# Down-projection weights kept as a bf16 copy in DRAM, and deeper prefetch around the norms, in a two-layer mLSTM/attention trunk

## The chip, the cores and the metric

One Trainium2 chip, one program on all 8 NeuronCores (two dies: cores 0 to 3 and 4 to 7). Each core computes one sequence of the batch, nothing is exchanged. The metric is the device time of the slowest core in microseconds. Executions come in two kinds. In *fast* ones every core holds nearly the full TensorE clock (a mean of 0.96 to 0.98 in the kernel before); in *slow* ones the cores of one die or of both are granted less (means down to 0.80). A ratio of two kernels here is the mean time of one kernel's fast runs over that of the other's fast runs of the same rounds, so it is not quite the ratio of the medians that are quoted beside it.

Because an execution can be slow in one stage and undisturbed in another, I also give *stage lengths at full clock*: from the first matmul of a stage to the first of the next, core by core, and the median over those cores whose record shows no throttling (a granted clock of about 0.81) in that stage. They can be compared between runs whose total times cannot.

The clock records hold three values: 1, 0.8125 (0.81 in the views) and 0.5. The last is the half clock of the prediction. On core 4 of the kernel before it is read from 1383.4 to 1407.3 us, around PE's waits of 6.8 and 13.2 us at the head of layer 0's first up stage.

## The reference, cut to what matters

Two layers. Layer 0 mixes tokens with an mLSTM, layer 1 with dilated sliding-window attention; after each comes a gated ConvFFN. Every sub-layer starts with an RMSNorm (with a scale and a shift from a conditioning vector) and ends with a residual add.

```python
for i in range(DEPTH):                       # 2
    h = rms_norm(x, norm_mix[i]) * (1.0 + sc_m) + sh_m
    y = mlstm_mixer(...) if i % 2 == 0 else dilated_mixer(...)
    x = x + g_m * y                          # y ends with "@ w_out", 2048 x 2048
    h = rms_norm(x, norm_ffn[i]) * (1.0 + sc_f) + sh_f
    x = x + g_f * conv_ffn(h, ...)           # up 2048 x 11264, conv, gate, down 5632 x 2048
return rms_norm(x, norm_out)
```

D = 2048, 2048 tokens a core, D_FF = 5632. All weights arrive as f32; the matmuls run on bf16 or f16.

## The kernel before

A recorder puts instructions on the five engines in program order and derives the semaphores. POOL, which computes and issues loads, and DVE work through their lists in that order (in the timeline that the prediction shows, POOL's add starts at 7901.47 us after a wait of 14.68 us, and its four loads only at 7902.68; DVE's eviction starts at 7899.73, behind a norm tile that waited 4.19 us). The stages are: prologue, mLSTM, output projection 0, FFN 0 (up, down for tokens 0 to 1023; up, down for 1024 to 2047), attention, output projection 1, FFN 1 (the same four). "First" and "second" up and down mean these token halves. The activations of a half stay in SBUF, so the down weights pass three times: once in the first down stage, twice in the second, which does one 512-token tile at a time.

The ring of weight slabs: six slots; POOL (GpSimd) issues a load as soon as PE has released a slot. The down slabs are cast from f32 to bf16 by the DMA itself.

```python
def load(self):                              # class slabs, cut
    ...
    if kind == "u":
        self.c.R.dma("pool", self.t[...][:], self.c.T["f_wu"][self.l, a, b], ...)
    else:
        self.c.R.dma("pool", self.td[...][:], self.c.T["f_wd"][self.l, a, b], ...)
```

Down stage, cut. Per output tile: 44 matmuls, eviction on DVE, square on ACT, row sum on POOL, then two or three steps of `bg`, the norm of the other token half, which runs in the shadow of this stage.

```python
for n_, (fo, ss) in enumerate(order):
    for q in range(4):
        w = ring.get(...)
        ...                                   # 11 matmuls per token tile
        ring.done()                           # POOL: loads the next slabs
    for s_ in ss:
        if m + 1 < 32: ldx(m + 1)             # residual, one tile ahead
        R.stt(n, PS[...], gcol[...], xin[m % 2][:], ALU.mult, ALU.add)      # DVE
        ...
        R.act(sq[m % 2][:], n, AF.Square)                                   # ACT
        R.tt("pool", a[:], a[:], sq[m % 2][:], ALU.add)                     # POOL
        bg = pull(bg, 2 if tb == 0 else 3)    # norm tiles: load, DVE, then ACT or a store
```

The norm loads one tile ahead into `len(xr)` buffers, two of them:

```python
    ld(0)
    for fc in range(16):
        if fc + 1 < 16: ld(fc + 1)
        R.stt(x[:], x[:], gvec[...], rstd, ALU.mult, ALU.mult)
        ...                                   # ACT into hT or B; in the last stage a store to outT
        yield
```

The output projections use the same pattern: residual and result on two buffers each, and the norm of the first token half beside the second half's matmuls.

The softmax here doesn't subtract the row's maximum and nothing guards it: scores larger than these inputs give would overflow.

## Time and profile before

| | us |
|---|---|
| five timed runs before the change was tried | 7680, 8241, 8354, 8452, 8489; median 8353.61 |
| profiled run (slow): die 0, die 1 | 8118, 8336 |
| output projections, full clock | 247.5 and 258.4 |
| first up stages | 554.0 and 554.1 |
| first down stages | 310.8 and 310.6 |
| second up stages | 536.1 and 536.0 |
| second down stages | 414.4 and 442.8 |

The stage rows are medians over undisturbed cores, layer 0 first. (The last second down stage also holds the 19 us end of the program.) The lines of the profile are shown in the prediction and not repeated.

### The profile page before, as it was taken

How to read it: one execution, taken by the hardware profiler on the slowest of the kernel's cores; microseconds unless marked ns; L12 is line 12 of the kernel's file. 1: busy time of each engine (PE TensorE's matmuls, PEld its weight loads, DVE VectorE, ACT ScalarE, POOL GpSimd, SP SyncE). 2: the span in 40 equal slices, each digit the busy share in tenths (PEclk: the TensorE clock that was granted, in tenths of full speed). 3: DMA queues.
4: the chain of work that ended last, by engine and by line, in shares of the span. 5: the costliest groups of instructions: out<-in, count | busy, mean ns of one | idle time of the engine just before them, and what ended most of it. 6: DMA issues, size and time to landing. Idle time of an engine off the chain costs nothing.

```text
span 8352.0 us, 123527 instructions; the slowest of 8 cores (8106.8 to 8352.0 us)
## 1 busy us (share of the span) xinstructions
PE 7827.3 (94%) x44026; PEld 4252.0 (51%) x44216; DVE 3892.7 (47%) x6968; ACT 2383.5 (29%) x4525; POOL 2107.6 (25%) x2931
## 2 busy tenths in 40 slices
PE   2799998999999888999999999999999999999978
PEld 2466653444444335776666666666434443444433
DVE  1656645883388422443333333433246661377511
ACT  2644433442144212222222222222133331133300
POOL 1322222222222222332222222222322221222222
PEclk9899999999999999998888888888778888888877
DMA  9067656556755795232222221111454446544588
GB/s 187 12 109 123 107 126 156 88 87 131 149 87 87 139 197 117 52 54 49 42 48 49 41 49 24 31 31 24 113 160 71 72 71 138 113 71 71 87 180 167
DMA packets 275358, 774.66 MB, mean 93 GB/s; under 512 B 30272, under 2 KB 31808, under 8 KB 268608
## 3 DMA queue, kind: packets, MB, share of 16 engines
q0 software_dynamic: 151056, 541.20, 38.9%
q1 hardware_dynamic: 123696, 225.54, 8.7%
q8 instruction: 361, 5.91, 0.3%
q14 instruction: 245, 2.01, 0.1%
HBM read 1229.37 MB, written 78.38 MB: 157 GB/s over the span
## 4 chain that ended last, share of the span: by engine, by line
PE 82%; DMA 9%; DVE 4%; issue 2%; ACT 2%; POOL 1%; another core or an unknown queue 0%; SPq 0%; DVEq 0%; ACTq 0%; POOLq 0%
PE PS L209 82%; DMA f_nx<-xb 2%; DMA outT<-f_nx 2%; DMA o_h<-xa 1%; DMA f_down<-f_wd 1%; DMA f_r<-sums 1%; DMA s_wa<-w_ada 1%; DMA o_x<-xT 0%; DMA f_x<-xb 0%; POOL s_scr L227 0%; DVE f_tv L223 0%; DVE f_tg L223 0%; DMA o_x<-xb 0%; DMA m_wab<-w_ada 0%
## 5 line engine op out<-in xcount | busy, mean ns | idle before, releaser
L209 PE MATMUL PS<-a_wa,hT 128*128 128x384 bf16 x12288 | 2421.0, 361 | 17.2 <-DVE a_R L237 17.2
L209 PEld LDWEIGHTS PS<-a_wa,hT 128*128 128x128 bf16 x12288 | 1455.8, 121 | 774.5 <-issue 22.5
L209 PE MATMUL PS<-f_act,f_down 128*128 128x512 bf16 x5516 | 1380.0, 415 | 104.9 <-DMA f_down<-f_wd 93.5
L209 PE MATMUL PS<-B,f_up 128*128 128x512 f16 x5632 | 1438.8, 408 | 7.0 <-DVE o_n L223 6.8
L209 PE MATMUL PS<-B,f_ws 128*128 128x512 f16 x4224 | 1103.3, 409 | 22.4 <-DVE f_ws L227 22.4
L209 PEld LDWEIGHTS PS<-f_act,f_down 128*128 128x128 bf16 x5632 | 587.1, 105 | 902.3 <-issue 594.4
L209 PEld LDWEIGHTS PS<-B,f_up 128*128 128x128 f16 x5632 | 582.0, 103 | 774.0 <-issue 443.6
L219 ACT ACTIVATE a_qkv<-PS 128x384 bf16<-128x384 f32 x768 | 377.1, 491 | 1999.1 <-PE PS L209 1999.1
L237 DVE COPY a_R<-PS 128x64 f32<-128x64 f32 x768 | 172.5, 225 | 1399.7 <-ACT a_qkv L219 1399.5
L209 PEld LDWEIGHTS PS<-B,f_ws 128*128 128x128 f16 x4224 | 437.1, 104 | 601.4 <-issue 354.4
L209 PE MATMUL PS<-m_wkvo,hT 128*128 128x320 bf16 x4096 | 622.2, 304 | 0.0
L227 POOL TENSOR_TENSOR f_act<-f_tg,f_tv 128x1024 bf16<-128x1024 f32 x176 | 413.4, 2349 | 713.1 <-DVE f_tv L223 538.7
L227 POOL TENSOR_TENSOR a_tA<-a_R,a_cs 128x128 f32<-128x128 f32 x384 | 174.7, 455 | 1362.5 <-DVE a_R L237 1335.0
L223 DVE SCALAR_TENSOR_TENSOR f_tv<-PS,f_cw,f_tv 128x1023 f32<-128x1023 f32 x352 | 451.1, 1281 | 141.8 <-ACT f_tv L219 119.7
L209 PE MATMUL PS<-yT,o_w 128*128 128x512 bf16 x2006 | 494.4, 411 | 14.1 <-DVE o_n L223 6.0
L227 DVE TENSOR_TENSOR PS<-PS,f_p 128x512 f32<-128x512 f32 x528 | 359.7, 697 | 284.4 <-PE PS L209 283.3
L209 PEld LDWEIGHTS PS<-m_wkvo,hT 128*128 128x128 bf16 x4096 | 401.7, 101 | 154.7 <-issue 1.8
L219 ACT ACTIVATE f_p<-PS 128x512 f32<-128x512 f32 x528 | 314.5, 596 | 570.6 <-PE PS L209 497.5
L223 DVE SCALAR_TENSOR_TENSOR f_tg<-PS,f_cw,f_tg 128x1023 f32<-128x1023 f32 x352 | 450.2, 1279 | 55.1 <-ACT f_tg L219 36.5
L204 POOL DMA_DIRECT2D f_up<-f_wu x352 | 197.4, 561 | 1067.6 <-PE PS L209 1041.2
L219 ACT ACTIVATE f_tg<-PS,f_cb,f_cw 128x1024 f32<-128x1024 f32 x176 | 212.0, 1205 | 766.2 <-DVE PS L227 766.2
L204 POOL DMA_DIRECT2D f_down<-f_wd x384 | 208.1, 545 | 720.5 <-PE PS L209 700.2
(184 smaller groups left out, 7406.7 us busy)
## 6 DMA issues: line engine op xcount, KB each, us to landing
f_up<-f_wu POOLq DMA_DIRECT2D x352, 512.0 KB, 5.1
f_down<-f_wd POOLq DMA_DIRECT2D x384, 352.0 KB, 7.4
a_wa<-a_wi POOLq DMA_DIRECT2D x48, 1536.0 KB, 10.5
m_wab<-w_ada POOLq DMA_DIRECT2D x64, 512.0 KB, 6.2
xa<-o_n SPq DMA_DIRECT2D x128, 256.0 KB, 2.3
f_x<-xa SPq DMA_DIRECT2D x128, 256.0 KB, 6.5
a_wab<-w_ada POOLq DMA_DIRECT2D x64, 512.0 KB, 5.2
xb<-f_n SPq DMA_DIRECT2D x96, 256.0 KB, 5.9
```

The lines of the kernel that those rows point to most:

```text
L204: self.q[eng].append((ws, lambda e, o=out, i=in_: e.dma_start(out=o, in_=i), sem))
L209: return self.op("pe", lambda e: e.matmul(out, lhsT=lhsT, rhs=rhs, start=start, stop=stop, **kw), [out], [lhsT, rhs])
L219: return self.op("act", lambda e: e.activation(**kw), outs, ins)
L223: return self.op("dve", lambda e: e.scalar_tensor_tensor(out=out, in0=in0, scalar=scalar, in1=in1, op0=op0, op1=op1), [out], ins)
L227: return self.op(eng, lambda e: e.tensor_tensor(out=out, in0=in0, in1=in1, op=op), [out], [in0, in1])
L237: return self.op(eng, lambda e: e.tensor_copy(out=out, in_=in_), [out], [in_])
```

## The change

The intent: load the down weights as bf16 by casting them once into DRAM, so that the second down stages stop being short of DMA; and give the norms and residuals around the matmul stages more buffers and earlier loads. Cut to its core (left out: new buffer addresses, one buffer for the squares of a down stage instead of two, and residual loads issued just after an eviction instead of just before it):

```diff
+    T["wdb"] = nc.dram_tensor("wdb", [2, 16, 4, 128, 11, 128], BF16, kind="Internal").ap()
@@ mLSTM, attention, first up stage of layer 0: one cast at a time
+def cast_down(c, l):
+    for fo in range(16):
+        for q in range(4):
+            c.R.dma("pool", c.T["wdb"][l, fo, q], c.T["f_wd"][l, fo, q], f"cast{q}", dw=[("wdb", l, fo, q)])
+            yield
@@ slabs.load
-            self.c.R.dma("pool", self.td[...][:], self.c.T["f_wd"][self.l, a, b], ...)
+            self.c.R.dma("pool", self.td[...][:], self.c.T["wdb"][self.l, a, b], ..., dr=[("wdb", self.l, a, b)])
@@ norm_tiles: loads len(xr) // 2 ahead
-    ld(0)
+    ah = len(xr) // 2
+    for fc in range(ah):
+        ld(fc)
     for fc in range(16):
-        if fc + 1 < 16:
-            ld(fc + 1)
+        if fc + ah < 16:
+            ld(fc + ah)
@@ phase_out: four buffers for residual, result and norm; residual three ahead
-    rst0, nx = hs[2:4], hs[4:6]
+    rst0, nx = hs[2:4], hs[4:6] + [... two more ...]
-    ldx(0)
+    for i in range(3):
+        ldx(i)
@@ phase_out, second token half, output tile 14: the first weight sums of the up stage
+                if fo == 14:
+                    first_sums(c, l)
@@ phase_ffn, norm of the other half
-            yield
-            yield
+            for _ in range(4):
+                yield
             rstd_of(c, rst[:], rst[:], ...)
-            yield from norm_tiles(c, n_li, n_src, tq, rst[:], nx, [0])
+            yield from norm_tiles(c, n_li, n_src, tq, rst[:], nx + xn if l == 1 and tb == 1 else nx, [0])
@@ phase_ffn, residual: three buffers, two ahead
-        ldx(0)
+        for i in range(2):
+            ldx(i)
```

More of the change, by code (lines that the diff above doesn't have):

```diff
@@ L167, in dma @@
         ins = [] if dr is None or dr else [in_]
-        if dw:
+        if in_.tensor.name in self.dram_names:
+            ins = []
+        elif dw:
             ins = [in_]
-        elif in_.tensor.name in self.dram_names:
-            ins = []
         val = self.dsem.get(sem, 0) + 16
@@ L840, in phase_mlstm @@
     feeder, bg = feeds(), ada_bg()
+    cast = cast_down(c, 0)
     for s in range(N + 2):
@@ L875, in phase_mlstm @@
                 M.load_w(h + 1, (tt // 3,))
+        if 2 <= s < 26:
+            cast = pull(cast)
+        c.cast0 = cast
         if s == 111:
@@ L945, in phase_out @@
     src, dst, li = (("xT", "xa", 2), ("xb", "xa", 3))[l]
-    XR = c.R2 + kb(64.25)
-    xin = [R.sb(f"o{l}_x{i}", [128, 512], F32, XR + 2048 * i) for i in range(2)]
-    xn = [R.sb(f"o{l}_n{i}", [128, 512], F32, XR + 4096 + 2048 * i) for i in range(2)]
+    xin = [R.sb(f"o{l}_x{i}", [128, 512], F32, a) for i, a in enumerate(
+        [c.HA + 2048 * k for k in range(4)] + [c.R1 + 4096 * k for k in (6, 7, 8, 9)])]
+    xn = [R.sb(f"o{l}_n{i}", [128, 512], F32, a) for i, a in enumerate(
+        [c.HA + kb(8) + 2048 * k for k in range(4)] + [c.R1 + 4096 * k for k in (10, 11, 12, 13)])]
+    xi = lambda m: m % 4 + 4 * (m >= 35)
     acc0 = [R.sb(f"o{l}_a{k}", [128, 512], F32, c.HA + kb(56) + 2048 * k) for k in range(2)]
-    sq = [R.sb(f"o{l}_q{k}", [128, 512], F32, c.HA + kb(60) + 2048 * k) for k in range(2)]
+    sq = [R.sb(f"o{l}_q{k}", [128, 512], F32, a) for k, a in enumerate((c.HA + kb(60), c.HA + kb(62), c.R1 + 4096 * 14, c.R1 + 4096 * 15))]
     hs = [R.sb(f"o{l}_h{k}", [128, 512], F32, c.R1 + 4096 * k) for k in range(6)]
     acc = [acc0, hs[0:2]]
-    rst0, nx = hs[2:4], hs[4:6]
+    rst0, nx = hs[2:4], hs[4:6] + [R.sb(f"o{l}_h{k}", [128, 512], F32, c.R2 + kb(54 + 2 * k)) for k in (6, 7)]
     xcnt = [0]
@@ L961, in ldx @@
         tq = tb * 2 + sub
-        R.dma("sp", xin[m % 2][:], T[src][:, fo, tq * 512:(tq + 1) * 512], f"xin{m % 2}", dr=[(src, fo, tq)])
-    ldx(0)
+        R.dma("sp", xin[xi(m)][:], T[src][:, fo, tq * 512:(tq + 1) * 512], f"xin{m % 4}", dr=[(src, fo, tq)])
+    for i in range(3):
+        ldx(i)
     bg = None
@@ L973, in phase_out @@
                     R.mm(PS[:, bk, :], W.w[fo][:, kc, :], c.yT[:, kc, sl], kc == 0, kc == 15)
-                if m + 1 < 64:
-                    ldx(m + 1)
-                n = xn[m % 2]
-                R.stt(n[:], PS[:, bk, :], gcol[:, fo:fo + 1], xin[m % 2][:], ALU.mult, ALU.add)
-                R.dma("sp", T[dst][:, fo, sl], n[:], f"st_x{m % 2}", dw=[(dst, fo, tq)])
+                n = xn[xi(m)]
+                R.stt(n[:], PS[:, bk, :], gcol[:, fo:fo + 1], xin[xi(m)][:], ALU.mult, ALU.add)
+                if m + 3 < 64:
+                    ldx(m + 3)
+                R.dma("sp", T[dst][:, fo, sl], n[:], f"st_x{m % 4}", dw=[(dst, fo, tq)])
                 a = acc[tb][sub]
@@ L982, in phase_out @@
                 else:
-                    q = sq[m % 2]
+                    q = sq[m % 2 + 2 * (m >= 35)]
                     R.act(q[:], n[:], AF.Square)
@@ L1002, in phase_out, with weight_sums, first_sums @@
         R.dma("sp", T["sums"][2 + sub], acc[1][sub][:], f"sums{sub}", dw=[("sums", 2 + sub)])
+def cast_down(c, l):
[3 more added lines that the diff above has]
+            yield
+def weight_sums(c, S, wg, wv, halves=(0, 1)):
+    R = c.R
+    a11, a12, a21, a22 = wg[:, 0:8, :], wg[:, 8:16, :], wv[:, 0:8, :], wv[:, 8:16, :]
+    if 0 in halves:
+        R.tt("dve", S[:, 0], a21, a22, ALU.add)
+        R.tt("dve", S[:, 1], S[:, 0], a11, ALU.subtract)
+    if 1 in halves:
+        R.tt("dve", S[:, 2], a12, S[:, 1], ALU.subtract)
+        R.tt("dve", a21, a11, a21, ALU.subtract)
+def first_sums(c, l):
+    c.wsum = [c.R.sb(f"f{l}_ws{i}", [128, 3, 8, 128], F16, (c.HA + kb(56), c.R2 + kb(60))[i]) for i in range(2)]
+    weight_sums(c, c.wsum[0], c.ring.get(0), c.ring.get(1))
 class slabs:
@@ L1009, in __init__ @@
         R = c.R
-        at = [c.R2 + kb(24) + 4096 * i for i in range(self.NR)]
-        self.t = [R.sb(f"f{l}_up{i}", [128, 16, 128], F16, a) for i, a in enumerate(at)]
-        self.td = [R.sb(f"f{l}_down{i}", [128, 11, 128], BF16, a) for i, a in enumerate(at)]
+        self.t = [R.sb(f"f{l}_up{i}", [128, 16, 128], F16, c.R2 + kb(24) + 4096 * i) for i in range(self.NR)]
+        self.td = [R.sb(f"f{l}_down{i}", [128, 11, 128], BF16, c.R2 + kb(24) + 4096 * i) for i in range(self.NR)]
         seq = []
@@ L1042, in load @@
         else:
-            self.c.R.dma("pool", self.td[self.slot[n]][:], self.c.T["f_wd"][self.l, a, b], f"ring{self.slot[n]}")
+            self.c.R.dma("pool", self.td[self.slot[n]][:], self.c.T["wdb"][self.l, a, b], f"ring{self.slot[n]}",
+                         dr=[("wdb", self.l, a, b)])
         self.last[self.slot[n]] = n
@@ L1065, in phase_ffn @@
     tv = R.sb(f"f{l}_tv", [128, 1024], F32, o + kb(56))
-    wsum = [R.sb(f"f{l}_ws{i}", [128, 3, 8, 128], F16, (c.HA + kb(56), o + kb(60))[i]) for i in range(2)]
+    wsum = c.wsum
     p1, p5, p16 = (R.sb(f"f{l}_p{i}", [128, 512], F32, a) for i, a in enumerate((c.HA + kb(62), o + kb(66), o + kb(68))))
@@ L1071, in phase_ffn @@
     assert o + kb(72.5) <= c.END
-    xin = [R.sb(f"f{l}_x{i}", [128, 512], F32, o + kb(64) + 2048 * i) for i in range(2)]
-    xn = [R.sb(f"f{l}_n{i}", [128, 512], F32, o + kb(60) + 2048 * i) for i in range(2)]
-    rst = R.sb(f"f{l}_r", [128, 512], F32, o + kb(68))
-    acc = [R.sb(f"f{l}_acc{i}", [128, 512], F32, o + kb(52 + 2 * i)) for i in range(2)]
-    nx = [R.sb(f"f{l}_nx{i}", [128, 512], F32, o + kb(56 + 2 * i)) for i in range(2)]
-    sq = [R.sb(f"f{l}_sq{i}", [128, 512], F32, o + kb(48 + 2 * i)) for i in range(2)]
+    d = [R.sb(f"f{l}_d{i}", [128, 512], F32, o + kb(48 + 2 * i)) for i in range(11)]
+    xin, xn, rst, acc, nx, sq = d[0:3], d[3:5], d[5], d[6:8], d[8:10], d[10]
     R.dma("sp", cw[:], T["f_cw"][:, l], "fcw")
@@ L1088, in mm8 @@
             R.mm(PS[:, bank, :], lhsT, B[:, quart, k, :], start and k == 0, k == 7, more=not start)
-    def weight_sums(j, wg, wv, half):
-        S = wsum[j % 2]
-        a11, a12, a21, a22 = wg[:, 0:8, :], wg[:, 8:16, :], wv[:, 0:8, :], wv[:, 8:16, :]
-        if half == 0:
-            R.tt("dve", S[:, 0], a21, a22, ALU.add)
-            R.tt("dve", S[:, 1], S[:, 0], a11, ALU.subtract)
-        else:
-            R.tt("dve", S[:, 2], a12, S[:, 1], ALU.subtract)
-            R.tt("dve", a21, a11, a21, ALU.subtract)
     def conv_base(j, p, t):
@@ L1124, in up @@
                 wg, wv = (ring.get(0), ring.get(1)) if j == 0 else (ring.get(2), ring.get(3))
-                if j == 0:
-                    weight_sums(0, wg, wv, 0)
-                    weight_sums(0, wg, wv, 1)
+                if j == 0 and tb == 1:
+                    weight_sums(c, wsum[0], wg, wv)
                 mm8(s4 + 2, wg, 0, B11, True)
@@ L1143, in up @@
             if j < 43:
-                wnext = (ring.get(2), ring.get(3))
-                weight_sums(j + 1, *wnext, 0)
-                weight_sums(j + 1, *wnext, 1)
+                weight_sums(c, wsum[(j + 1) % 2], ring.get(2), ring.get(3))
             if j > 0:
@@ L1149, in up @@
                 R.tt("pool", act[:, pv, :], tg[pv % 2][:], tv[:], ALU.mult)
+                if l == 0 and tb == 0:
+                    c.cast0 = pull(c.cast0)
             if j == 44:
@@ L1187, in ldx @@
             tq = tb * 2 + s_
-            R.dma("sp", xin[m % 2][:], T[src][:, fo, tq * 512:(tq + 1) * 512], f"xin{m % 2}", dr=[(src, fo, tq)])
-        ldx(0)
+            R.dma("sp", xin[m % 3][:], T[src][:, fo, tq * 512:(tq + 1) * 512], f"xin{m % 3}", dr=[(src, fo, tq)])
+        for i in range(2):
+            ldx(i)
         slot[0] = 0
@@ L1206, in phase_ffn @@
                 sl = slice(tq * 512, (tq + 1) * 512)
-                if m + 1 < 32:
-                    ldx(m + 1)
                 n = xk[:, fo, s_ * 512:(s_ + 1) * 512] if last else xn[m % 2][:]
-                R.stt(n, PS[:, s2 + s_, :], gcol[:, fo:fo + 1], xin[m % 2][:], ALU.mult, ALU.add)
+                R.stt(n, PS[:, s2 + s_, :], gcol[:, fo:fo + 1], xin[m % 3][:], ALU.mult, ALU.add)
+                if m + 2 < 32:
+                    ldx(m + 2)
                 if not last:
@@ L1216, in phase_ffn @@
                 else:
-                    R.act(sq[m % 2][:], n, AF.Square)
-                    R.tt("pool", a[:], a[:], sq[m % 2][:], ALU.add)
+                    R.act(sq[:], n, AF.Square)
+                    R.tt("pool", a[:], a[:], sq[:], ALU.add)
                 m += 1
@@ L1225, in phase_ffn @@
                     s_ = ss[0]
-                    bg = final_norm(c, acc[s_], rst, xk, s_) if last else second(c, li, dst, 2 + s_, acc[s_], rst, (nx, xin)[s_])
+                    bg = final_norm(c, acc[s_], rst, xk, s_) if last else second(c, li, dst, 2 + s_, acc[s_], rst, nx)
                 if l == 0 and n_ == 29:
@@ L1424, in phase_attn @@
     c.out_w = out_weights(c, 1)
+    cast = cast_down(c, 1)
     for n in range(NU + 14):
+        if n >= 64 and n % 8 == 4:
+            cast = pull(cast)
         if n < NU:
```

## The prediction

> **What bounds the kernel now.** I read the list of cores first, then the page, then busy time by stage, and only then the waits and the order of instructions inside the worst stage.
>
> ```profile
> die 0 (median of its cores): 8117.8 us, clock 0.911
> die 1 (median of its cores): 8335.9 us, clock 0.881
> ...
> PE 7827.3 (94%) x44026; PEld 4252.0 (51%) x44216; DVE 3892.7 (47%) x6968; ACT 2383.5 (29%) x4525; POOL 2107.6 (25%) x2931
> q0 software_dynamic: 151056, 541.20, 38.9%
> q1 hardware_dynamic: 123696, 225.54, 8.7%
> ```
>
> The profiled run is in the slow state, and so are four of the five timed runs (8240 to 8489 us; the fast one took 7680). TensorE is busy 94% of the span: only its idle time and its half-clock time can be won. I therefore cut the program at the changes of matmul operand. Core 4's record runs at full clock until about 3200 us and at 0.81 after; core 0's is the other way round. First core 4 (output projection, FFN up, down, up, down of layer 0; last row: the final stage, throttled), then core 0 at full clock (output projection, up, down, up, down of layer 1; last row: what follows the last projection matmul). Columns: from:to, length, busy time of PE, PEld, DVE, ACT, POOL, clock, DMA share, GB/s.
>
> ```profile
> 1134.10:1385.10 251.00, 227.23 (x1007) 101.95 (x1027) 85.00 (x123) 62.08 (x96) 73.52 (x62) 0.96 0.69 185
> 1385.10:1939.40 554.30, 540.99 (x2486) 244.15 (x2488) 442.88 (x574) 230.23 (x270) 156.32 (x138) 0.98 0.53 90
> 1939.40:2250.60 311.20, 302.48 (x1364) 137.10 (x1391) 59.90 (x97) 46.67 (x68) 71.37 (x93) 0.98 0.71 156
> 2250.60:2786.20 535.60, 534.68 (x2476) 241.89 (x2476) 453.90 (x656) 218.11 (x265) 151.99 (x134) 1.00 0.53 88
> 2786.20:3200.20 414.00, 329.48 (x1376) 140.49 (x1403) 71.04 (x86) 61.22 (x88) 104.73 (x154) 0.91 0.91 183
> 7895.40:8352.00 456.60, 382.32 (x1378) 155.63 (x1404) 74.25 (x100) 28.18 (x43) 106.50 (x153) 0.77 0.84 171
> ```
>
> ```profile
> 6028.80:6289.40 260.60, 231.45 (x1031) 102.33 (x1028) 87.49 (x129) 61.92 (x95) 81.03 (x73) 0.96 0.67 184
> 6289.40:6844.40 555.00, 540.42 (x2486) 243.95 (x2487) 442.08 (x574) 230.26 (x270) 157.60 (x140) 0.98 0.54 91
> 6844.40:7155.00 310.60, 303.99 (x1392) 137.13 (x1391) 60.13 (x97) 46.68 (x68) 71.28 (x93) 0.98 0.73 156
> 7690.60:8129.90 439.30, 330.05 (x1406) 140.62 (x1404) 74.24 (x101) 28.73 (x43) 106.11 (x154) 0.88 0.85 179
> 8111.20:8129.90 18.70, 2.04 (x2) 0.47 (x2) 10.69 (x16) 1.32 (x2) 0.00 (x0) 0.50 0.58 224
> ```
>
> The second up stage is the yardstick: 44 x 56 = 2464 matmuls in 535.6 us at clock 1.00, 217.4 ns each, nothing lost. Output has 64 x 16 = 1024 matmuls (222.6 us), down 32 x 44 = 1408 (306.1 us). Losses at full clock, layer 0 then layer 1: output 28 and 38, first up 19 and 19, first down 5 and 5, second down 108 and 133 (of which 19 are the end of the program). About 336 us in all; the second down stages hold most of it. The waits and order there (core 0, layer 1):
>
> ```profile
> DVE f_nx L223 <- DMA f_nx<-xb: 157.7, 27, 12.6
> POOL f_acc L227 <- ACT f_sq L219: 157.6, 27, 16.7
> PE PS L209 <- DMA f_down<-f_wd: 66.9, 19, 9.3
> PE PS L209 <- DMA f_r<-sums: 21.1, 2, 18.8
> ...
> 7899.06 0.75 DVE L223 SCALAR_TENSOR_TENSOR f_nx<-f_nx,g_nrm,f_r 128x512 f32<-128x512 f32 x1 [4.19 <-DMA f_nx<-xb]
> 7899.73 0.74 DVE L223 SCALAR_TENSOR_TENSOR f_xk<-PS,g_modT,f_x 128x512 f32<-128x512 f32 x1
> 7900.63 0.63 ACT L219 ACTIVATE f_sq<-f_xk 128x512 f32<-128x512 f32 x1 [17.42 <-DVE f_xk L223]
> 7901.47 1.26 POOL L227 TENSOR_TENSOR f_acc<-f_acc,f_sq 128x512 f32<-128x512 f32 x1 [14.68 <-ACT f_sq L219]
> 7902.68 2.17 POOL L204 DMA_DIRECT2D f_down<-f_wd  x4
> ```
>
> PE waits for f_down, but these four loads were issued late: POOL issues them in order behind its add, the add waits for ACT's square, that for DVE's eviction, and DVE stands behind three norm tiles that wait for their loads from xb. Such a round takes about 19 us there, against 44 x 217 ns = 9.6 us of matmuls.
>
> [...]the f32 weights come through q0. From the two queue lines, an engine writes 541.20 MB/(0.389 x 16 x 8352 us) = 10.4 GB/s on q0 and 225.54/(0.087 x 16 x 8352) = 19.4 on q1, which does not cast[...]. [...]a load from xb takes some 4 us, and 9 to 10 where it meets a burst of four f_down loads. [...]the throttled half here reads 0.81.
>
> **The change part by part.**
> 1. Down weights are cast once into a bf16 copy in DRAM (64 slabs a layer; layer 0: 24 in the mLSTM, 40 in its first up stage; layer 1: in attention) and then loaded three times as bf16. A second down stage loads 128 slabs of 360 KB, 46.1 MB: now 46.1/10.4/16 = 277 us of all 16 engines. Layer 0 has 112 transfers of 262 KB on q1 beside it, 29.4/19.4/16 = 95 us; 372 of 414 is 0.90, the table has 0.91. After: 46.1/19.4/16 = 149 (estimate), plus 95, is 244 of about 320, 0.76. A burst of four slabs shrinks from 8.7 to 4.6 us and with it the slow load from xb.
> 2. Casts cost 128 x 360 KB/10.4 GB/s/16 = 2.2 us of DMA each and about 0.55 us of POOL issue (f_down's row: 545 ns), 70 us of POOL in all, in stages where the matmul queue has DMA to spare (0.2 to 0.55). On the path: 0 to 5 us.
> 3. The final stage's norm gets four buffers and loads two ahead. Now two buffers alternate load, multiply, store: (4.5 + 0.75 + 4.5)/2 = 4.9 us a tile with the median landings there, 15 for three, more in a burst; with four 7.3, below 9.6. Layer 0's norm keeps two buffers: load plus 0.75 plus ACT 0.72 over two. At 7.9 us landing it is 4.7 a tile, 14 for three (its rounds are 14 us); it needs a landing under 4.9, and I expect 4 to 5: just enough.
> 4. Four yields instead of two before the sums' matmul: the f_r waits (52 us in 6 times over the program) go to the next tile, hidden.
> 5. Output stage: residual loads three ahead instead of one, four buffers each way, norm loads two ahead. First weight sums move ahead of the last output tile, which takes the 13 to 14 us wait for f_ws, and its half-clock tail, out of the first up.
> No matmul is added or removed.
>
> Recovered at full clock: output 22 + 27, first up 16 + 16, first down 4 + 4, second down 95 + 100: 284 us. Left over: the starts, a few norm waits of layer 0, the 19 us end. Fast: 7680 - 284 = 7396.
>
> At 0.81 a matmul takes 217.4/0.8125 = 267.6 ns and covers more: core 4's final stage loses 456.6 - 376.8 - 19 = 61, I take back 50 per second down and 5 elsewhere, about 105. A slow run has each die throttled for about half: (284 + 105)/2 = 195, 8354 - 195 = 8159.
>
> **Rivals.** (a) Layer 0's norm stays the bound: landings stay above 6 us, rounds near 11 to 12 for 11 of 32 tiles; costs 25 us back. For it: only two buffers. Against it: the burst halves. (b) The casts disturb: DRAM to DRAM has no sample here; if each took 10 us of queue, the up stage's loads, 2 slabs per 12 us, would starve, 40 rounds x 3 = 120 us lost. Against it: the share there is 0.53 and slabs lie a round ahead. (c) The weights were hidden anyway and only the buffers count: then the gain holds except layer 0's second down, about 190. (d) Denser matmuls bring more throttling: the fast state gets rare and slow runs gain only 100.
>
> **Range and chances.** Fast I expect 7396 (7350 to 7460), slow 8159 (8030 to 8290). By four of five I take the median to fall in the slow state: 8155 us. The range must hold both states: 7360 to 8290. Fast against fast is -3.7%; falling short of 2% (154 us) needs (b) or most terms to fail: faster 0.94, same 0.05, slower 0.01.
>
> **What would show it.** Right: second down near 315 to 320 and 330 us at full clock, its DMA share about 0.76, no f_r waits, POOL's f_down bursts gone, first up within 3 us of 535.6, output near 230. Wrong: f_nx waits of layer 0 as before (3), up stage with f_up waits (2), output still waiting on o_x (5).

## More of the kernel before

Undisturbed cores of one run lie 1 to 10 us apart in a stage (about 2 us in the first down stages, up to 9 in the outputs and the second down stages), so a difference of 2 us between medians says little where the cores overlap.

A few down matmuls are issued between the last up matmuls. They count to the up stage, since I cut at the last change of operand (core 4 before; start us, us):

```profile
1933.13 4.70 PE L209 MATMUL PS<-f_act,f_down 128*128 128x512 bf16 x21
1937.67 1.89 PE L209 MATMUL PS<-B,f_up 128*128 128x512 f16 x8
```

So a first up stage holds 22 down matmuls and a second one 11 (a record or so can be missing from a trace), which the down stages lack.

## The result

Median 7526.88 us (10 runs, 7392.72 to 8722.87). The kernel before, in 18 runs, has a median of 7698.5 (7679.89 to 8907.96). Fast against fast: **ratio 0.9616**, 95% interval 0.9605 to 0.9628, so 3.84% faster. The output is correct. Five of the ten runs were fast, 7392.7 to 7398.1 us.

The profiled run was slow, on one die only. From its list of cores:

```profile
die 0 (median of its cores): 7881.5 us, clock 0.919
die 1 (median of its cores): 7392.3 us, clock 0.986
```

Die 1 ran undisturbed, so core 4 can be set beside the full-clock rows of before. Busy time by stage of the changed kernel, core 4, columns as in the prediction: output, first up, first down and second down of layer 0; first up and second down of layer 1.

```profile
1131.40:1357.90 226.50, 223.56 (x1007) 101.10 (x1027) 82.15 (x123) 61.75 (x96) 73.20 (x62) 0.99 0.73 204
1357.90:1908.30 550.40, 540.33 (x2485) 243.94 (x2487) 445.48 (x574) 229.92 (x270) 176.84 (x178) 0.99 0.64 117
1908.30:2209.20 300.90, 299.43 (x1363) 136.35 (x1390) 60.31 (x97) 46.35 (x68) 71.62 (x93) 1.00 0.55 162
2746.00:3065.50 319.50, 307.30 (x1377) 138.87 (x1404) 63.91 (x86) 61.11 (x88) 104.39 (x154) 0.98 0.77 237
5680.10:6223.40 543.30, 539.71 (x2487) 243.81 (x2487) 438.63 (x569) 227.35 (x266) 151.12 (x134) 0.99 0.52 89
7061.90:7390.50 328.60, 304.85 (x1378) 138.09 (x1404) 76.53 (x101) 28.62 (x43) 106.67 (x154) 0.97 0.75 239
```

Layer 0's second down stage went from 414 to 319.5 us, and its DMA share from 0.91 to 0.77: it is no longer full. Queue q0 carries the weight slabs. In that stage of core 4, before and after (packets, MB, share of the 16 engines):

```profile
q0 software_dynamic: 17993, 46.26, 66.5%
q0 software_dynamic: 10039, 46.14, 48.7%
```

That is 275 us of all 16 engines before (277 in the prediction) and 156 after (149 estimated): an engine wrote 10.5 GB/s of its recorded busy time with the cast and 18.5 without it, on the same queue. Why the cast costs that much is not shown. Layer 0's norm loads landed in 7.9 us before and 4.9 after (medians of 48), just the 4.9 that part 3 of the prediction asked for.

The first down stage is now 300.9 us on every undisturbed core, with nothing lost: 1386 matmuls at 215.8 ns from start to start, and two short ones for the row sums, 0.86 us each. The 215.8 ns hold in dense stretches of up and down stages, in both kernels.

The waits in the final stage of core 4:

```profile
DVE f_d L223 <- DMA f_d<-xb: 45.3, 18, 4.6
POOL f_d L227 <- ACT f_d L219: 40.6, 28, 8.2
```

Before they were 157.7 and 157.6 us, and PE waited 66.9 us for f_down; now no such line is there. (The changed kernel names its buffers f_d.) The order of instructions in that stage shows why:

```profile
7130.59 1.26 POOL L227 TENSOR_TENSOR f_d<-f_d,f_d 128x512 f32<-128x512 f32 x1 [0.83 <-ACT f_d L219]
7131.80 0.56 POOL L204 DMA_DIRECT2D f_down<-wdb  x1
7133.98 0.54 POOL L204 DMA_DIRECT2D f_down<-wdb  x1 [1.62 <-PE PS L209]
```

Here POOL's add waits 0.8 us where it waited 15, and the f_down loads are no longer issued in a burst of four: after the first, each waits until PE frees a slot. The norm's loads themselves did not get faster in this stage (median landing 4.5 us before, 6.1 after); it is the two more buffers that hide them, as experiment 4 will show. The page's list of DMA issues (KB each, median us to landing) has the new transfers:

```profile
f_down<-wdb POOLq DMA_DIRECT2D x384, 352.0 KB, 4.0
wdb<-f_wd POOLq DMA_DIRECT2D x128, 352.0 KB, 4.6
```

f_down landed in 7.4 us before. Full-clock stage lengths, medians:

| stage | before | after | recovered | predicted |
|---|---|---|---|---|
| output 0, 1 | 247.5, 258.4 | 225.9, 231.6 | 21.6, 26.8 | 22, 27 |
| first up 0, 1 | 554.0, 554.1 | 549.4, 543.6 | 4.6, 10.5 | 16, 16 |
| first down 0, 1 | 310.8, 310.6 | 300.9, 300.9 | 9.9, 9.7 | 4, 4 |
| second up 0, 1 | 536.1, 536.0 | 537.8, 537.2 | -1.7, -1.2 | 0, 0 |
| second down 0, 1 | 414.4, 442.8 | 320.4, 328.1 | 94.0, 114.7 | 95, 100 |
| mLSTM, attention | 942.7, 2382.6 | 943.0, 2382.1 | -0.3, 0.5 | 0, 0 |

The sum is 289 us, against 284 predicted and against 7680 - 7395 = 285 from the fast runs.

### The profile page after: what moved, and what is told of

Read it like the earlier page. It is cut to its first block, busy times and chain, and to the rows that moved or that the text cites.

```text
span 7904.3 us, 123847 instructions; the slowest of 8 cores (7388.7 to 7904.3 us)
## 1 busy us (share of the span) xinstructions
PE 7543.2 (95%) x44026; PEld 4194.8 (53%) x44216; DVE 3897.6 (49%) x6968; ACT 2379.5 (30%) x4525; POOL 2177.8 (28%) x3059
## 4 chain that ended last, share of the span: by engine, by line
PE 86%; DMA 4%; DVE 4%; issue 2%; POOL 2%; ACT 2%; DVEq 0%; SPq 0%; POOLq 0%; ACTq 0%
PE PS L209 86%; DMA s_wa<-w_ada 1%; DMA f_d<-xb 1%; DMA m_wab<-w_ada 1%; POOL yT L227 0%; DVE a_accD L240 0%; POOL s_scr L227 0%; DMA o_h<-xa 0%; DVE f_tv L223 0%; DMA o_x<-xT 0%; POOL a_qkv L227 0%; DVE f_tg L223 0%; POOL a_tB L227 0%; DVE m_og L240 0%; DMA f_down<-wdb 0%
## 5 line engine op out<-in xcount | busy, mean ns | idle before, releaser
L209 PE MATMUL PS<-a_wa,hT 128*128 128x384 bf16 x12288 | 2203.6, 338 | 14.5 <-DVE a_R L237 14.5
L209 PEld LDWEIGHTS PS<-a_wa,hT 128*128 128x128 bf16 x12288 | 1433.0, 119 | 596.1 <-issue 18.8
L209 PE MATMUL PS<-f_act,f_down 128*128 128x512 bf16 x5516 | 1343.5, 408 | 21.4 <-DMA f_down<-wdb 10.8
L204 POOL DMA_DIRECT2D f_down<-wdb x384 | 208.0, 542 | 779.4 <-PE PS L209 754.1
```

What stands on the lines that cost most here:

```text
L204: self.q[eng].append((ws, lambda e, o=out, i=in_: e.dma_start(out=o, in_=i), sem))
L209: return self.op("pe", lambda e: e.matmul(out, lhsT=lhsT, rhs=rhs, start=start, stop=stop, **kw), [out], [lhsT, rhs])
```

## The experiments

All twelve kernels gave correct results. Experiments 1 to 4, 5 to 8 and 9 to 12 ran on three different chips, each time beside 11 runs of the kernel before. On the first chip no run of any kernel had the full clock, the kernel before included (11 runs, 8142 to 8906 us). So experiments 1 to 4 are read by stage lengths at full clock alone, from those cores and stages that were undisturbed. "After" below is the changed kernel.

**1. The bf16 copy alone.** The kernel before with `wdb`, the casts and the new slab load; every buffer as before.

```diff
  (before)
+ T["wdb"], cast_down and its three call sites
-   ... self.c.T["f_wd"][self.l, a, b] ...
+   ... self.c.T["wdb"][self.l, a, b] ..., dr=[("wdb", self.l, a, b)]
```

> The kernel before plus only the bf16 copy of the down weights; every buffer and prefetch as before. My theory (cheaper weights and more buffers each take part of the second down stages): layer 0's second down about 335 us at full clock (changed kernel 319.5, before 414), because its norm has two buffers in both kernels and only the f_r waits come back; layer 1's about 385 (328 and 439), because two buffers at about 4.5 us per landing still need 14.6 us for three norm tiles against 9.4 us of matmuls. Outputs 251 and 261 as before. Fast time about 7547 us, ratio 0.983. Rival (c), the weights were hidden anyway: both second downs as before, 7650 to 7680, ratio above 0.996.

Both second down stages of core 6 (layer 0, layer 1):

```profile
2934.40:3267.30 332.90, 312.44 (x1404) 139.36 (x1403) 64.52 (x83) 60.55 (x88) 103.88 (x153) 0.96 0.73 226
7460.20:7827.10 366.90, 316.37 (x1406) 139.90 (x1404) 74.22 (x100) 28.16 (x43) 105.59 (x153) 0.94 0.68 213
```

Medians, of two cores each, 332.2 and 368.1: the copy alone takes 82 and 75 us out of the two stages. Rival (c) falls: the weights were not hidden. In layer 1 some 40 us stay although the DMA share is only 0.68: another wait took over. The first down stages stay at 309.0 and 309.5 (310.8 and 310.6 before): there the copy is worth almost nothing. My 385 for layer 1 was 17 too high.

**2. The buffers alone.** After, with the slabs loaded as f32 again and no casts.

```diff
  (after)
- T["wdb"] load, cast_down call sites
+   ... self.c.T["f_wd"][self.l, a, b] ...
```

> The changed kernel without the bf16 copy: down weights cast on load again, three times. My theory: both second downs become bound by the DMA engines, 277 us for weights plus 95 to 108 for the rest, so about 395 us in layer 0 and 410 in layer 1; first down back to about 310. Fast time about 7560 us, ratio to the kernel before 0.984. Rival (c): the buffers do it all but for layer 0's second down, time about 7490 or less, layer 1's second down under 345.

Second down stages of core 4:

```profile
2901.20:3307.50 406.30, 331.03 (x1377) 140.09 (x1404) 67.55 (x83) 60.93 (x88) 104.41 (x154) 0.92 0.93 185
7450.10:7863.10 413.00, 326.60 (x1378) 136.23 (x1404) 75.39 (x101) 28.65 (x43) 106.33 (x154) 0.93 0.94 190
```

406.1 and 412.4 as medians, with a DMA share of 0.93 and 0.94: with f32 slabs the buffers leave these stages little room, by the 372 us of DMA work that I had estimated for layer 0 from the queues' rates (10.4 and 19.4 GB/s). Buffers alone recover 8 and 30 us. First down: 300.9 in both layers, where I had expected 310. So the first down stage gains from something in the buffers part, not from the copy.

**3. The casts alone.** Experiment 2 with the 128 casts issued and never read.

```diff
  (experiment 2)
+ T["wdb"], cast_down and its three call sites, slabs still from f_wd
```

> As e2, but the 128 casts into DRAM are issued at the places where the changed kernel has them and their result is never read (down weights are still loaded as f32). The difference to e2 is the price of the casts by themselves. My theory: 0 to 5 us, with layer 0's first up stage within 2 us of that of e2. Rival (b), the casts disturb the up stage's loads: 20 to 120 us more than e2, in the first up stage of layer 0.

mLSTM 945.4 us against 941.4 in experiment 2 (ranges over the cores 940.1 to 950.3 and 940.5 to 945.5, so within the spread), attention 2382.6 against 2381.3. The stage that I had named, the first up of layer 0, was throttled in both runs and cannot be read there. The changed kernel's own record settles it for core 4. PE waits 10.9 us in that stage, 8.7 of them for f_ws and the rest for ACT and an eviction, all in its first 20 us. In the other 530 us, with casts going on throughout, PE waits for nothing. Rival (b) falls there; in the mLSTM a cost of up to 5 us cannot be told from nothing.

**4. Two buffers in the final norm.**

```diff
  (after)
-   ... nx + xn if l == 1 and tb == 1 else nx, [0])
+   ... nx, [0])
```

> The changed kernel with two instead of four buffers for the norm in the final stage (loads then one ahead). My theory: load, multiply and store alternate over two buffers again, 4.9 us a tile at 4.5 us per landing, 14.6 us for three against 9.4 us of matmuls over 11 of the 32 output tiles: layer 1's second down about 328 + 50 = 378 us, fast time about 7446 us. If instead the bf16 weights alone had freed that stage: within 5 us of the changed kernel's 7396.

Layer 1's second down stage: 372.4 us, 44 more than after. All else is unchanged (layer 0's: 317.8). Waits there, core 6:

```profile
POOL f_d L227 <- ACT f_d L219: 120.6, 28, 12.3
DVE f_d L223 <- DMA f_d<-xb: 114.7, 27, 9.3
...
PE PS L209 <- DMA f_down<-wdb: 26.3, 7, 5.7
```

and what the DMA-issuing SP waits for, among it the stores that must empty a buffer before the next norm load:

```profile
SPq L270 <- DMA outT<-f_d: 110.0, 28, 6.4
```

(48.5 us in 17 waits in the changed kernel's core 4.) This is the plainest case of a wait that bears the wrong name. The weights are the same cheap bf16 slabs as in the changed kernel, and yet PE waits for f_down: POOL issues them late behind its add, the add waits for ACT's square, and DVE stands at norm tiles whose buffers are still being stored. Two more 256 KB buffers end it.

**5. Two steps ahead of the row sums instead of four.**

```diff
  (after)
-            for _ in range(4):
-                yield
+            yield
+            yield
```

> The changed kernel with two instead of four steps between the load of the row sums and the matmul that needs it. My theory: the waits of PE for f_r return, some 7 us in each first down stage and two of 2 to 10 us in each second one plus the half-clock time after each: first downs 307 to 309 us at full clock (changed kernel 300.9), second downs 5 to 15 us longer than 320 and 328. About 7425 us if fast. Rival, the bf16 weights alone made the first down shorter: they stay at 301.

First down stages 309.2 and 309.8 (after: 300.9 both), second ones 329.6 and 332.2 (320.4, 328.1): 30 us in all; the one fast run took 7435.3. The wait in the first down stage of core 4:

```profile
PE PS L209 <- DMA f_d<-sums: 5.6, 1, 5.6
```

One wait of 5.6 us costs the stage 8.3: its mean clock is 0.99 where the changed kernel's is 1.00. So 8.3 and 8.9 of the 9.9 and 9.7 us come from the two steps, and the rival (the bf16 weights did it) falls, as it did in 1 and 2; the 1 to 2 us left are what the copy gave there in experiment 1.

**6. Residual of the output stage one tile ahead.**

```diff
  (after, phase_out)
-    for i in range(3):
-        ldx(i)
+    ldx(0)
-                if m + 3 < 64:
-                    ldx(m + 3)
+                if m + 1 < 64:
+                    ldx(m + 1)
```

> The changed kernel with the residual of the output stage loaded one tile ahead instead of three (buffers and norm loads unchanged). My theory: most of the gain of the output stages goes back: 240 to 248 us and 250 to 258 us at full clock instead of 226 and 232. Rival, the norm loads two ahead did it: outputs within 4 us of the changed kernel.

Outputs 229.6 and 236.5 (after 225.9, 231.6): only 3.7 and 4.9 back, where I expected 14 to 26. The first ups grow to 552.0 and 550.5 (549.4, 543.6; in layer 0 the cores of the two runs overlap). Ratio to before 0.9638 (0.9619 to 0.9658), after 0.9616. My theory of the output stage fell; the rival, the norm loads, was taken to experiments 9, 10 and 12.

**7. The first weight sums at the head of the up stage.**

```diff
  (after)
-                if fo == 14:
-                    first_sums(c, l)
@@ phase_ffn
-                if j == 0 and tb == 1:
+                if j == 0:
                     weight_sums(c, wsum[0], wg, wv)
```

> The changed kernel with the first weight sums formed at the head of the first up stage, as before. My theory, which the result has already lowered (first ups 549 and 544 us instead of the 539 I predicted): the sums cost about 3 us of VectorE plus the half-clock tail, so first ups 551 to 556 us at full clock, up to 12 us per layer. Rival, the wait at the head is the late residual loads and not the sums: no difference to the changed kernel.

(The buffers of the sums move back with them.) First ups 549.8 and 543.5 us against 549.4 and 543.6: no difference (the one fast run took 7403.7). PE's wait for f_ws in layer 0's first up, core 4, in the changed kernel:

```profile
PE PS L209 <- DVE f_ws L227: 8.7, 1, 8.7
```

and here:

```profile
PE PS L209 <- DVE f_ws L227: 10.6, 1, 10.6
```

In the changed kernel's order of instructions DVE reaches the early sums only at 1365.0 us, after seven evictions that each waited for a late residual load: the up stage's matmuls began at 1357.9. Moving the sums earlier in DVE's queue did nothing here, where the queue itself was late. This is the part of the change that gained nothing by itself.

**8. A try at a version that beats both.** Attention's first weight tile in four parts over the last three output tiles, attention's next weights later, first sums two tiles earlier.

```diff
  (after)
-                if fo == 14:
+                if fo == 12:
                     first_sums(c, l)
@@ end of layer 0's second down: k-tiles 0-3, 4-7, 8-11, 12-15 of the first attention weight tile
-                if l == 0 and n_ == 29: c.attn_pre()
+                (part 0 after tile 29, part 1 inside tile 30, part 2 after it, part 3 inside tile 31)
@@ phase_attn
-    ada_load(LO); ada_load(LO + 1)          # ahead of the loop
-        if n == 2: c.att_load(1)
+        if n == 7: c.att_load(1)
+        if n == 11: ada_load(LO); ada_load(LO + 1)
```

> A version meant to beat both: the changed kernel with attention's first weight tile loaded in four parts over the last three output tiles of layer 0's second down stage, attention's next weight loads issued some 13 to 20 us later so that the last norm loads do not queue behind them, and the first weight sums two output tiles earlier. Expected at full clock: layer 0's second down 308 us (320), attention 2368 (2382), first ups 542 and 541 (549 and 544); about 7362 us if fast, ratio to the kernel before 0.9587 (changed kernel 0.9616). If these were not what holds PE there: within 5 us of the changed kernel.

Layer 0's second down fell to 313.6 us (320.4), but attention rose to 2386.2 (2382.1), and the first ups came to 546.7 and 545.7 (549.4, 543.6). From output 0 on, the stage medians sum to some 4 us less, which is within the spread of the cores; the one fast run took 7396.9. No gain that can be shown. The wait at the head of attention had not gone (9.5 us on core 4, 10.2 in the changed kernel); that the weight load met the same norm loads at step 7 is my reading and was not tested by itself.

**9. Norm of the output stage on two buffers.**

```diff
  (after, phase_out)
-    rst0, nx = hs[2:4], hs[4:6] + [... two more ...]
+    rst0, nx = hs[2:4], hs[4:6]
```

> The changed kernel with the output stage's norm on two buffers, loads one ahead, as before; residual loads stay three ahead on four buffers. Loading the residual one ahead had cost only 3.7 and 4.9 us, so the theory is now that the norm loads make the output stage's gain: outputs about 243 and 252 us at full clock (226 and 232 in the changed kernel, 247.5 and 258 before) and first ups 551 to 554. Rival, the number of buffers for residual and result did it: outputs within 4 us of the changed kernel.

Outputs 241.1 and 244.8 us (after 225.9, 231.6; before 247.5, 258.4): 15 and 13 of the 22 and 27 us go back. Core 4, output 0:

```profile
1129.10:1370.10 241.00, 226.21 (x1007) 101.78 (x1027) 79.95 (x123) 62.12 (x96) 73.55 (x62) 0.97 0.68 191
```

Ratio 0.9653 (0.9633 to 0.9673). Read the other way, this kernel has the residual's part of the change alone: it gains 6 and 14 us over the kernel before. In layer 0 the norm's part is the larger one by far; in layer 1 the residual's part alone makes half of the gain.

**10. Residual and result on two buffers, norm as in the change.**

```diff
  (experiment 6)
-    xi = lambda m: m % 4 + 4 * (m >= 35)
+    xi = lambda m: m % 2 + 4 * (m >= 35)
     ... semaphores m % 2
```

> The changed kernel with two buffers each for residual and result in the output stage and residual loads one ahead, so as before but for the norm, which keeps four buffers and loads two ahead. If the norm loads make the gain: outputs 230 to 236 and 236 to 242 us at full clock, first ups 552 to 556 because the last residual loads come late. Rival, the buffers did it: outputs 243 and 252 or more.

Outputs 229.1 and 235.4, first ups 551.5 and 550.5; ratio 0.9635 (0.9619 to 0.9651). Hardly different from experiment 6: the number of residual buffers matters little, and what their depth gives is 3 to 4 us of each output stage and 2 and 7 us at the head of each first up.

**11. Second try at a better version.** As 8, with the sums back at tile 14 and attention's loads at steps 11 and 15.

```diff
  (experiment 8)
-        if n == 7: c.att_load(1)
-        if n == 11: ada_load(LO); ada_load(LO + 1)
+        if n == 11: c.att_load(1)
+        if n == 15: ada_load(LO); ada_load(LO + 1)
```

> Second try at a version that beats both. Attention's first weight tile stays in four parts (it shortened layer 0's second down from 320 to 313.6 us); attention's next loads now start at its step 11 and 15, after the last norm tile, because at step 7 they met the norm loads again (attention 2386 instead of 2382); weight sums where the changed kernel has them. Expected: second down 314, attention 2368 to 2374, about 7380 us if fast, ratio to the changed kernel 0.998. If the wait at the head of attention is not those loads: attention stays at 2382 and the time at 7390.

Second down 315.3 us, attention 2381.3. Three fast runs, 7393.8 to 7403.8; ratio to before 0.9613 (0.9597 to 0.9630), the same as the changed kernel's. In the record of core 4 the 10 us wait of step 10 is gone, but the last norm loads, issued at about the time of that weight load, took 12 us to land, and a 9 us wait appears 50 us into the stage. What it would take to clear the head of attention is left open.

**12. Only the norm loads of the output stage, on the kernel before.**

```diff
  (before)
-    rst0, nx = hs[2:4], hs[4:6]
+    rst0, nx = hs[2:4], hs[4:6] + [... two more ...]
@@ norm_tiles: loads len(xr) // 2 ahead, as in the change
```

> The kernel before with one edit: the output stage's norm gets four buffers and loads two tiles ahead. If the norm loads make the output stage's gain: outputs 230 to 236 and 238 to 244 us at full clock (247.5 and 258 before), all else as before, 7680 - 35 = about 7645 us if fast. Rival, it takes the residual buffers as well: outputs within 5 us of before.

Outputs 228.4 and 238.9 us against 247.5 and 258.4; everything else as before. Three fast runs, 7652.1 to 7664.0; ratio 0.9948 (0.9931 to 0.9966), a gain of 0.5% from a few lines: "same" by the 2% rule, but clear of 1. Core 4, output 0:

```profile
1135.70:1366.50 230.80, 224.29 (x1007) 101.30 (x1027) 85.21 (x123) 61.98 (x96) 74.17 (x62) 0.99 0.75 203
```

So most of the gain of the output stages can be had from the norm alone, four buffers and loads two ahead (the two were never separated): added alone it recovers 19 of 22 and 20 of 27 us, taken away alone it costs 15 and 13. In layer 1 the two parts overlap, since the residual's part alone recovers 14 of the 27.

## Why the prediction was right or wrong

**Wrong: the time given for the changed kernel.** The step that failed is "By four of five I take the median to fall in the slow state: 8155 us". It was drawn from five runs of the kernel before, four of them slow. The runs showed in its place: 5 of the 10 runs of the changed kernel were fast and the median was 7526.88, between a fast and a mildly slow run; of the 18 runs of the kernel before, 11 were fast. In the three groups of experiments, each on another chip, the kernel before alone gave 0, 7 and 6 runs of 11 at full clock. The share of slow runs changes that much from group to group; what sets it is not shown, and five runs of one group were no ground for the next ten. Because of this step the line states a change of 8155 to 8354, -2.4%, while the same text had derived -3.7% for fast runs, and -3.84% was measured.

**Wrong: what a slow run is.** "A slow run has each die throttled for about half" was read off one profiled run. Slow runs of the changed kernel went from 7656 to 8723 us; in the slowest the cores of one die stood at a mean clock of 0.82 and those of the other at 0.98 to 0.99 and about 7385 us. There is no one slow time to predict. At 0.81 a few stages can be read: output 272.6 us, first up 652.7, first down 366.0, final stage 392.1, against 275.7, 666.4, 375.2 and (core 4) 456.6 before, so 3, 14, 9 and 64 us recovered where I allowed 50 for the last and 5 for the others together. The gain under throttling was set too low. A matmul took 262.6 ns there from start to start (core 4 before), not 267.6. What a whole slow run gains cannot be told, since the lists of cores show no two throttled alike.

**Right: the fast time.** 7396 predicted, 7394.7 the mean of the five fast runs; the chance of 0.94 was put on the right side. That it fits within 2 us is partly luck: the terms were off by +12 (first down), +14 (second down), -17 (first up) and -3 us (second up), and these nearly cancel.

**Right: the second down stages, both size and mechanism.** 95 + 100 us predicted, 94.0 + 114.7 measured; the DMA share of 0.76 came out at 0.77 and 0.75. Experiment 1 gives the copy 82 and 75 us of it, experiment 2 the rest of the change 8 and 30, experiment 4 the four final buffers 44 on top of the cheap weights. The copy's price in engine time, 275 to 156 us, was foreseen too. The claim that PE's waits for f_down were in part POOL's late issue stands on experiment 4. The slow loads from xb are in the record as well, if not quite at the "9 to 10" us given: in the last stage of core 0 before, the nine issued within 3.5 us of the start of a burst of four f_down loads landed after 7.6 to 9.9 us (two of them above 9), most of those between such bursts after 2.8 to 4.5. Rivals (a), (b) and (c) all fell: layer 0's norm on two buffers kept pace (320 us, not 345), the casts cost the up stage nothing, the weights were not hidden.

**Right in the sum, wrong in its terms.** *First down*: 4 + 4 predicted, 9.9 + 9.7 measured. My yardstick was wrong: I divided the up stage by its 2464 up matmuls and left out the down matmuls in it. Both kinds start every 215.8 ns, and a first down stage holds 1386 matmuls and not 1408. Its least time is 300.9 us and not 306.1, so 5 us more were lost than I saw, and experiment 5 puts 8 to 9 of the 10 us on the row-sum wait (step 4 of the prediction, which I had sized too small there). *First up*: 16 + 16 predicted, 4.6 + 10.5 measured. The step "takes the 13 to 14 us wait for f_ws, and its half-clock tail, out of the first up" failed: on core 4 the wait only fell from 13.2 to 8.7 us in layer 0, and experiment 7 shows that moving the sums does nothing. In the order of instructions the sums stand behind evictions that wait for late residual loads. Experiments 6 and 10 give 7 of layer 1's 10.5 us to the residual's depth. Why the residual loads are late in layer 0 stays open. *Output*: 22 + 27 predicted and 21.6 + 26.8 measured, but I gave no share to the parts, and before experiment 6 I had the wrong one in front: it is mostly the norm loads, and in layer 1 either part alone recovers half or more. *Left out*: the second ups got 1 to 2 us longer.

Of rival (d), that denser matmuls make the fast state rarer, nothing can be said: 5 of 10 against 11 of 18 is no difference with so few runs.

## What to carry to other kernels

Where one engine both computes and issues loads, a late operand upstream can show as "PE waits for the weights": here POOL's four loads went out behind an add that had waited 14.7 us, and PE's waits for f_down in that stage, layer 1's second down, came to 66.9 us (core 0 before). Before buying bandwidth, look at when the load was issued, and before adding buffers, add up whether the DMA engines have the time at all. In layer 1's second down both were short, and experiments 1, 2 and 4 show that each cure alone leaves a good part of the loss; in layer 0's the copy alone brought 82 of 94 us. Before moving an instruction earlier, see whether its queue is itself late (experiment 7: 549.8 against 549.4 us). And where a chip has a throttled state, predict and compare in the undisturbed one, stage by stage if need be.
